# The last layer's modulation moved from attention's projections into the recurrence of the layer before

## The chip, the cores and the metric

One core of a Trainium2 chip runs the whole program. Five engines work side by side, each with its own queue in order: TensorE (PE; its weight loads are shown as PEld), VectorE (DVE), ScalarE (ACT), GpSimd (POOL) and SyncE (SP), which issues the DMAs. The metric is the device time of one execution in microseconds (us); less is better. The time of a kernel is the median of its runs.

## What is computed

A network of a first block and four layers over 512 tokens of width 1024, with 256 tokens of context beside them. The four layers are a gated convolution (0), an RWKV recurrence (1), attention (2) and a gated convolution again (3). Each layer has a modulation: shift, scale and gate, 3072 numbers for the token stream and 3072 for the context, from a vector that is the same in all layers.

```python
def modulation(cvec, w, b):
    m = jax.nn.silu(cvec) @ w + b          # cvec 1024, w 1024 x 3072
    return jnp.split(m, 3, axis=-1)

for i in range(4):
    shift, scale, gate = modulation(c, mod_w[i], mod_b[i])
    h = modulate(rmsnorm(x, norm_g[i]), shift[:, None], scale[:, None])
    ...                                     # layer i's branch gives y
    x = x + gate[:, None] * y
```

So the modulation of a layer depends on no layer before it, and can be computed at any time ahead of the layer that uses it. The modulation's weights are 12.6 MB a layer. Layer 1's recurrence runs over 12 blocks of 64 tokens, forward and backward at once:

```python
sa = jnp.einsum("bhvk,bhk->bhv", S, -kk_t)
S = (S * d_t[:, :, None, :] + sa[..., None] * (kk_t * a_t)[:, :, None, :]
     + v_t[..., None] * k_t[:, :, None, :])
out = jnp.einsum("bhvk,bhk->bhv", S, inp[5])
```

## The kernel before, in words

**The modulation.** A layer's 3072 columns are 24 blocks of 128. `mod_load` (line 597) loads one block of the weights, 512 KB, into a tile `mraw` of the pool `mods`, which has two buffers. `mod_mul` (lines 613 and 614) multiplies it: eight products of 128 x 32 by 128 x 128 in full fp32, four side by side in the columns of the array, and one ScalarE copy of the rows to `mrow`. After each four blocks `mod_cols` (lines 623 and 624) turns four rows into columns with four products, and VectorE adds the bias. `fill` does one such portion; `wblock`, which fetches and splits a block of any layer's weights, calls `fill` first, so the modulation is spread over a layer's weight blocks. `open_mods(to)` opens the pool and sets how far it goes; `close_mods` does what is left.

The layers 0 to 2 have their modulation computed in the first block and in the first convolution. Layer 3's is opened in `attn_layer`, just ahead of attention's projections, and interleaved with their 48 weight blocks. Its result is used only by the last convolution.

**The recurrence.** Each block j of 64 tokens needs four things in order: the scores (`scores`, line 1310, evicted by ScalarE as `Df`, line 1317, and by VectorE as `SK`, line 1319), a row recursion on VectorE that inverts small triangles (`rows`, lines 1343 and 1345), a block inverse on TensorE (`first`, line 1378, and `horner`, line 1387, from the tiles `T` and `M`), and the chain itself: `chain_v`, `chain_g` and `chain_u` (lines 1411, 1421, 1433) give U, which ScalarE and VectorE copy into `UV` (lines 1435 and 1436), `chain_s` (line 1443) makes the next state from it, `chain_o` (lines 1459 and 1466) the output. `step(j)` does the chain of block j, the block inverse of block j+1 and the scores and rows of block j+2, and starts the loads of `F` and `AR` of block j+3 (line 1284) and of V of block j+1 (line 1293). PSUM is split into two pools of four banks that go round: `pp` for scores, inverse and transposes, `pch` for the chain.

Steps -1 to 8 stand in `manual_schedule`: on each engine their instructions keep the order in which they are written. Steps 9 to 11, and all else, are ordered by a scheduler that simulates the program and gives each engine what is ready, by priority. Beside the last steps stand the normalization of one more row tile and the first weight blocks of the readout (`rwkv_w_o_2`), which starts with transposes on line 1654.

**Attention's projections.** 48 weight blocks of 512 KB are loaded (line 186), split by ScalarE and VectorE into a high and a low part (lines 170 and 173) and multiplied: keys, values and queries on lines 218 to 220, the gate on lines 199 to 202. The lines of the recurrence around the change are

```python
            sc(0, 1)
            if ch and j < 11:
                load_v(j + 1)
                for d in range(2):
                    chain_s(j, d)
```

Of the kernel before, what the change touches and what calls it, by code (L numbers as in the profile page):

```python
# [10 lines left out]
F32 = mybir.dt.float32  # L11
# [7 lines left out]
P = 128  # L19
# [15 lines left out]
WB=3  # L35
AP=[int(c) for c in "11"]
LT=2
MS=9
CB=4
CK=256  # L40
# [29 lines left out]
class K:  # L70
# [529 lines left out]
    def mod_mul(self):  # L600

        nc = self.nc
        i, j = divmod(self.mods_done, 24)
        self.mods_done += 1
        if j == 0:
            self.mods[i] = self.const.tile([P, 24, 2], F32, name=f"mod{i}")
        if j % 4 == 0:
            self.mod_rows = self.mpool.tile([P, 4, P], F32, name="mrow", bufs=1)
        raw = self.mraw.pop(0)
        ps = self.ptr.tile([P, 512], F32, name="tr")  # L610
        for k in range(KT):
            g = k % 4 * 32
            nc.tensor.matmul(ps[g:g + 32, 0:P], self.sc[:, k, :], raw[:, k, :], start=k < 4, stop=k >= 4)  # L613
        nc.scalar.activation(self.mod_rows[:, j % 4, :], ps[:, 0:P], AF.Copy)

    def mod_cols(self):

        nc = self.nc
        i, j = divmod(self.mods_out, 24)
        self.mods_out += 4  # L620
        ps = self.ptr.tile([P, 512], F32, name="tr")
        for q in range(4):
            nc.tensor.matmul(ps[:, 2 * q:2 * q + 2], self.mod_rows[:, q, :], self.msel, start=True, stop=True)
        nc.vector.tensor_tensor(self.mods[i][:, j:j + 4, :], ps[:, 0:8].rearrange("p (j s) -> p j s", s=2),
                                self.col("mod_b_2", 24 * i + j, 4).unsqueeze(2).to_broadcast([P, 4, 2]), ALU.add)

    def fill(self):

        if self.mods_done == self.mods_out + 4:
            self.mod_cols()  # L630
        if self.mods_read < self.mods_to:
            self.mod_load()
        if len(self.mraw) > 1 or self.mods_read == self.mods_to and self.mraw:
            self.mod_mul()

    def open_mods(self, to):

        self.mods_to = 24 * to
        self.mes = ExitStack()
        self.mpool = self.pool(self.mes, "mods", bufs=2, side="right")  # L640

    def close_mods(self):
        while self.mods_out < self.mods_to:
# [318 lines left out]
    def rwkv_layer(self, X, XC):  # L962
# [76 lines left out]
        def lerp_k(n, k, hi, lo):  # L1039
            t = stg.tile([P, WH], F32, name="l32", bufs=LT)  # L1040
            nc.vector.scalar_tensor_tensor(t, xx[:, k, :], self.col("rwkv_mu_2", 8 * n + k), h[:, k, 1:WH + 1],
                                           ALU.mult, ALU.add)
            self.split_x(hi, lo, t, True)
# [54 lines left out]
        def feat(name, i, shape=(P, 384)):  # L1098
            return fp.tile(list(shape), F32, name=name, bufs=FB[i])
# [3 lines left out]
        def done_k(p, t):  # L1103
            DQ(nc, 0).dma_start(k_d[p], t)
            sq = stg.tile([P, WH], F32, name="l32", bufs=LT)[:, :TA]
            hi, lo = [feat(nm, i, (P, WH))[:, :TA].bitcast(F32R) for nm, i in (("F", 5), ("AR", 6))]
# [180 lines left out]
        def load_v(j):  # L1287

            s = st[j]
            s.UV = []  # L1290
            for d in range(2):
                UV = B.pb.tile([P, H, 64], F32, name=f"UV{d}", bufs=2)
                nc.sync.dma_start(UV[hs[1 - d]].rearrange("p u v -> p (u v)"), vc_d[s.c[d] * 64:(s.c[d] + 1) * 64, :])
                nc.gpsimd.memset(UV[hs[d]], 0.0)
                s.UV.append(UV)
# [187 lines left out]
        def aside(j, i):  # L1483
            for _ in range(NAS[i][j]):
                next(normed, None)

        def step(j):

            ch, p2, p1 = j >= 0, 0 < j + 1 < 12, j + 2 < 12
            sc = (lambda d, g: scores(j + 2, d, g)) if p1 else (lambda d, g: None)  # L1490
            if p1:
                prep0(j + 2)
            if p2:
                expand(j + 1)
            if ch:
                G = chain_g(j)
            sc(0, 0)
            if ch:
                for hh in range(2):
                    chain_u(j, hh, G[hh])  # L1500
            sc(0, 1)
            if ch and j < 11:
                load_v(j + 1)
                for d in range(2):
                    chain_s(j, d)
            for g in range(4):
                if p2:
                    if g < 2:
                        first(j + 1, g)
                    else:  # L1510
                        horner(j + 1, 0, g - 2)
                if g % 2 == 0:
                    sc(1, g // 2)
                if g == 1:
                    if j + 3 < 12:
                        load(j + 3)
                    aside(j, 0)
            if p1:
                blocks(j + 2)
            for i in range(4):  # L1520
                if p2:
                    horner(j + 1, 1 + i // 2, i % 2)
                if p1:
                    rows(j + 2, max(1, 4 * i), 4 * i + 4)
                    tokens(j + 2, i // 2, i % 2)
                if ch and i < 3:
                    chain_o(j, i)
                if i == 2:
                    aside(j, 1)
            if p1:  # L1530
                back(j + 2)
            if j < 11:
                chain_v(j + 1)
            aside(j, 2)
# [48 lines left out]
        for nh in range(2):  # L1583
# [4 lines left out]
            def done_v(j, t, ps, nh=nh, lnb=lnb):  # L1588
# [7 lines left out]
                nc.vector.tensor_scalar(m, m, 1.0 / 64.0, None, ALU.mult)  # L1596
                vc = stg.tile([P, WH], F32, name="l32", bufs=LT)[:, :512].rearrange("p (h v) -> p h v", v=64)
                nc.vector.tensor_tensor(vc, p3, bc(m), ALU.subtract)
# [15 lines left out]
        zer = B.pb.tile([P, 512], mybir.dt.bfloat16, name="zer")  # L1614
        nc.gpsimd.memset(zer, 0.0)
        load_v(0)
        with tc.manual_schedule():
            for j in range(-1, MS):
                step(j)
            for _ in normed:  # L1620
                pass
        for j in range(MS, 12):
            step(j)
        lng = b0.tile([P, D], F32, name="lng", tag="SK00")
        nc.sync.dma_start(lng, ins["rwkv_ln_g_2"].rearrange("o n -> (o n)").partition_broadcast(P))
        for t in early[2:]:
# [9 lines left out]
        with ExitStack() as es:  # L1636
# [6 lines left out]
            for t in early + late:  # L1643
# [7 lines left out]
                for q in range(2):  # L1651
                    ps = self.ptr.tile([P, 512], F32, name="tr")
# [26 lines left out]
    def attn_layer(self, X, XC):  # L1679
# [7 lines left out]
        with ExitStack() as esl:  # L1687
# [7 lines left out]
            V = [kvp.tile([P, 6, HD], F32, name="V", bufs=8) for _ in range(8)]  # L1695
            rq = kvp.tile([P, 4, 16], F32, name="rq")
            kq = self.pool(esl, "atkq", bufs=2, side="right")
            self.open_mods(4)
            hds = [Ctx() for _ in range(16)]

            def split(hi, lo, x):
# [39 lines left out]
            with es_h:  # L1741
# [79 lines left out]
                for blk in range(8):  # L1821
                    gt = wk.tile([P, 2, T], F32, name="gt", tag="gt")
                    for m in range(2):
                        ps = self.mm()
# [1 line left out]
                        nc.scalar.activation(gt[:, m], ps, AF.Silu)  # L1826
                    nc.sync.dma_start(g_d[2 * blk:2 * blk + 2].rearrange("h d t -> d h t"), gt)

            self.close_mods()
            self.pes.close()  # L1830
            ylp = self.pool(esl, "atyl", bufs=8, side="right")
            with ExitStack() as es:
# [90 lines left out]
            with ExitStack() as es:  # L1923
# [3 lines left out]
                for nh in range(2):  # L1927
                    nsl = slice(nh * 512, (nh + 1) * 512)
                    self.linear_tm(w_out, nh * 512, lambda k: Gated(k, 0), lambda k: Gated(k, 1), TILES,
                                   lambda j, t, ps, nsl=nsl: self.residual(work, gate, X, j, nsl, ps), kts=16,  # L1930
# [141 lines left out]
```

## Time and profile before

| | us |
|---|---|
| median of 3 runs | 2657.45 |
| lowest and highest | 2656.79, 2659.92 |
| the profiled execution | 2661.63 |
| its span, first to last instruction | 2659.7 |
| TensorE busy | 2388.7 (90%) |
| VectorE, ScalarE, GpSimd busy | 1653.5, 1096.2, 589.7 |

The span is cut into stretches by the lines that run in them: the start of the recurrence from about 1240 us, the hand-ordered steps 0 to 8 up to about 1558, the last three steps up to 1638, the readout and attention's norm, and attention's projections from 1757 to 2096. A busy share says little by itself: what a stage is worth is read from what its last engine waits for.

### The profile page before, as it was taken

The numbers are of one execution on the slowest core, as the hardware profiler recorded it, in microseconds if no ns is written. First come the engines' busy times: TensorE is split into PE (matmuls) and PEld (weight loads), VectorE is DVE, ScalarE is ACT, GpSimd is POOL, SyncE is SP. The second block draws the span as 40 slices with busy tenths as digits, with TensorE's granted clock in tenths as the row PEclk, the third lists the DMA queues.
The fourth block names the chain that finished last, engine by engine and source line by source line (L and its number), as shares of the span: only waits on it lengthen the run. The fifth ranks groups of instructions, "written<-read, shape, count | busy, mean of one in ns | idle before, by whom it ended". The sixth has DMA issues, their size and how long they took to land. (4 is left out here: it accounts for less than half of the span.)

```text
span 2659.7 us, 48444 instructions
## 1 busy us (share of the span) xinstructions
PE 2388.7 (90%) x19868; PEld 1889.9 (71%) x19868; DVE 1653.5 (62%) x2580; ACT 1096.2 (41%) x2029; POOL 589.7 (22%) x544
## 2 busy tenths in 40 slices
PE   6998889899896889998799886989999899997997
PEld 4786667777575767666678775768788788876655
DVE  4434366995456478888788773554163478448836
ACT  4642353111434456653455552243233467432223
POOL 0101001000204046654232441110000387100001
PEclk8998899899997999997899997989999999998998
DMA  6533543434322237775433445242545311222331
GB/s 170 150 88 103 158 128 87 106 96 119 90 74 79 76 115 224 212 218 173 139 129 130 146 137 191 103 129 87 152 148 153 119 48 41 80 87 72 88 97 56
DMA packets 352941, 319.05 MB, mean 120 GB/s; under 512 B 19679, under 2 KB 292032, under 8 KB 352208
## 3 DMA queue, kind: packets, MB, share of 16 engines
q1 hardware_dynamic: 352720, 315.95, 39.6%
q8 instruction: 157, 2.57, 0.4%
q14 instruction: 64, 0.52, 0.1%
HBM read 241.85 MB, written 64.63 MB: 115 GB/s over the span
## 5 line engine op out<-in xcount | busy, mean ns | idle before, releaser
L173 DVE TENSOR_TENSOR wlo<-wraw,whi 128x1024 fp32r<-128x1024 f32 x212 | 263.6, 1244 | 460.9 <-ACT whi L170 453.4
L170 ACT ACTIVATE whi<-wraw 128x1024 fp32r<-128x1024 f32 x212 | 224.2, 1058 | 644.0 <-PE mm L200 336.0
L200 PE MATMUL mm<-hT_lo,whi 128*128 128x512 f32 (+1 forms) x864 | 323.5, 375 | 0.0
L199 PE MATMUL mm<-hT_hi,whi 128*128 128x512 f32 (+1 forms) x864 | 319.5, 381 | 2.5 <-ACT h L710 1.0
L202 PE MATMUL mm<-hT_hi,wlo 128*128 128x512 f32 (+1 forms) x864 | 290.7, 372 | 0.4 <-DVE wlo L173 0.4
L837 DVE SCALAR_TENSOR_TENSOR cvo<-ypad,dwh,cvo 128x784 f32<-128x784 f32 (+1 forms) x270 | 236.7, 906 | 4.7
L202 PEld LDWEIGHTS mm<-hT_hi,wlo 128*128 128x128 f32 x864 | 164.0, 190 | 40.6 <-issue 2.0
L199 PEld LDWEIGHTS mm<-hT_hi,whi 128*128 128x128 f32 x864 | 164.7, 191 | 38.6 <-issue 12.8
L200 PEld LDWEIGHTS mm<-hT_lo,whi 128*128 128x128 f32 x864 | 164.5, 191 | 32.7 <-issue 5.4
L218 PE MATMUL mm<-whi,hT_hi 128*128 128x512 f32 x384 | 152.6, 398 | 1.3 <-ACT hT_hi L263 1.3
L219 PE MATMUL mm<-wlo,hT_hi 128*128 128x512 f32 x384 | 152.3, 397 | 0.0
L220 PE MATMUL mm<-whi,hT_lo 128*128 128x512 f32 x384 | 150.1, 399 | 0.0
L797 POOL MEMSET ypad<- 128x15 f32 x16 | 1.8, 114 | 494.5 <-DVE cvo L837 272.1
L200 PE MATMUL mm<-llo,whi 128*128 128x256 f32 (+1 forms) x256 | 89.7, 368 | 11.3 <-DVE llo L273 11.3
L199 PE MATMUL mm<-lhi,whi 128*128 128x256 f32 (+1 forms) x256 | 85.0, 369 | 6.2 <-ACT lhi L270 6.2
L218 PEld LDWEIGHTS mm<-whi,hT_hi 128*128 128x128 f32 x384 | 72.5, 189 | 18.4 <-issue 1.8
L1317 ACT ACTIVATE Df<-ps 32x128 f32<-32x128 f32 x176 | 68.2, 387 | 37.9 <-PE ps L1310 35.7
L218 PE MATMUL mm<-whi,lhi 128*128 128x512 f32 x192 | 80.2, 424 | 4.0 <-DVE so L1566 3.2
L219 PEld LDWEIGHTS mm<-wlo,hT_hi 128*128 128x128 f32 x384 | 72.5, 189 | 15.6 <-issue 1.0
L220 PEld LDWEIGHTS mm<-whi,hT_lo 128*128 128x128 f32 x384 | 71.8, 189 | 16.5 <-issue 2.4
L613 PE MATMUL tr<-mraw,sc 128*32 128x128 f32 x1536 | 67.4, 291 | 16.8 <-DMA mraw<-in_mod_w_dram 13.6
L219 PE MATMUL mm<-wlo,lhi 128*128 128x512 f32 x192 | 79.9, 416 | 1.8 <-DVE wlo L173 1.8
(523 smaller groups left out, 5822.1 us busy)
## 6 DMA issues: line engine op xcount, KB each, us to landing
mraw<-in_mod_w_dram SPq DMA_DIRECT2D x96, 512.0 KB
wraw<-in_conv_w_in_dram SPq DMA_DIRECT2D x48, 512.0 KB
wraw<-in_attn_w_in_dram SPq DMA_DIRECT2D x48, 512.0 KB
wraw<-in_w_in_dram SPq DMA_DIRECT2D x24, 512.0 KB
f_d<-F SPq DMA_DIRECT2D x32, 384.0 KB
ar_d<-AR SPq DMA_DIRECT2D x32, 384.0 KB
F<-f_d SPq DMA_DIRECT2D x24, 512.0 KB
AR<-ar_d SPq DMA_DIRECT2D x24, 512.0 KB
```

Of the source, the lines that this page charges most:

```text
L170: nc.scalar.activation(hi[:, :n], raw, AF.Copy)
L173: nc.vector.tensor_tensor(lo[:, :n], raw, hi[:, :n].bitcast(F32), ALU.subtract)
L199: nc.tensor.matmul(ps[s], wh[:, k, :], xh(k)[:, a:b], start=k == 0, stop=False)
L200: nc.tensor.matmul(ps[s], wh[:, k, :], xl(k)[:, a:b], start=False, stop=False)
L202: nc.tensor.matmul(ps[s], wl[:, k, :], xh(k)[:, a:b], start=False, stop=k == kts - 1)
L218: nc.tensor.matmul(ps, h, wh[:, kk, :], start=k == 0, stop=False)
L219: nc.tensor.matmul(ps, h, wl[:, kk, :], start=False, stop=False)
L220: nc.tensor.matmul(ps, l, wh[:, kk, :], start=False, stop=k == kts - 1)
L613: nc.tensor.matmul(ps[g:g + 32, 0:P], self.sc[:, k, :], raw[:, k, :], start=k < 4, stop=k >= 4)
L797: nc.gpsimd.memset(yp_[:, 0:15], 0.0)
L837: nc.vector.scalar_tensor_tensor(acc, yp_[:, tap:tap + W], dwh[:, tap, kt:kt + 1], acc, ALU.mult, ALU.add)
L1317: nc.scalar.activation(s.Df[rows, :, :, gsl].rearrange("p t a u -> p u a t"), p3[rows, :, 32 * b:32 * b + 32].rearrange("p u (a t) -> p u ...
```

## The change

Layer 3's modulation is no longer opened in attention. It is opened just ahead of the recurrence's steps, with one buffer for `mraw` instead of two, and each step calls a new `fill_one` as often as a table `MODS` says, between the last scores of the first direction and the two state products. `fill_one` does, in this order, a due turn into columns, the product of the loaded block, and the load of the next. In the recurrence the products take their bank from the pool `pp`. One `fill_one` ahead of the steps only loads. The table gives two to step -1, one to each of steps 0 to 8, then three, five and five; a last call behind step 11 does the last turn.

```diff
+MODS=(2, 1, 1, 1, 1, 1, 1, 1, 1, 1, 3, 5, 5)
...
-        ps = self.ptr.tile([P, 512], F32, name="tr")
+        ps = self.mbank()
...
+    def mbank(self):
+        return self.ptr.tile([P, 512], F32, name="tr")
+
+    def fill_one(self):
+
+        if self.mods_done == self.mods_out + 4:
+            self.mod_cols()
+        if self.mraw:
+            self.mod_mul()
+        if self.mods_read < self.mods_to:
+            self.mod_load()
...
-    def open_mods(self, to):
+    def open_mods(self, to, bufs=2):
...
-        self.mpool = self.pool(self.mes, "mods", bufs=2, side="right")
+        self.mpool = self.pool(self.mes, "mods", bufs=bufs, side="right")
...
             if ch and j < 11:
                 load_v(j + 1)
+            for _ in range(MODS[j + 1]):
+                self.fill_one()
+            if ch and j < 11:
                 for d in range(2):
                     chain_s(j, d)
...
         load_v(0)
+
+        self.open_mods(4, 1)
+        self.mbank = lambda: bank("pp")
+        self.fill_one()
         with tc.manual_schedule():
...
         for j in range(MS, 12):
             step(j)
+        while self.mods_out < self.mods_to:
+            self.fill_one()
+        self.mes.close()
+        del self.mbank
...
             kq = self.pool(esl, "atkq", bufs=2, side="right")
-            self.open_mods(4)
...
-            self.close_mods()
             self.pes.close()
```

## Rows read from the trace of the kernel before

**Rows 1.** Busy time by stretch: length, busy us by engine, PEclk, DMA share, GB/s
```profile
1295.00:1558.00 263.00, 236.56 (x6357) 206.98 (x6353) 208.91 (x494) 142.46 (x329) 97.28 (x103) 0.94 0.41 132
1558.00:1638.00 80.00, 60.88 (x1693) 52.61 (x1691) 47.50 (x90) 32.16 (x68) 18.55 (x18) 0.89 0.33 103
...
1757.00:1990.00 233.00, 233.00 (x1394) 186.56 (x1393) 101.58 (x182) 77.65 (x206) 6.58 (x5) 1.00 0.43 126
1990.00:2096.00 106.00, 106.00 (x482) 87.62 (x480) 36.32 (x49) 35.47 (x51) 4.78 (x4) 1.00 0.52 154
```

**Rows 2.** Waits, 1757 to 2100: waiter <- releaser, us, times, longest (PE, ACT)
```profile
PE sc L1857 <- ACT gt L1826: 1.5, 1, 1.5
...
ACT whi L170 <- PE mm L220: 84.5, 29, 8.3
```

**Rows 3.** Timeline of PE in the projections: start, us, line, operation, count
```profile
1867.28 0.39 PE L220 MATMUL mm<-whi,hT_lo 128*128 128x512 f32 x1
1867.51 0.39 PE L218 MATMUL mm<-whi,hT_hi 128*128 128x512 f32 x1
1867.83 0.64 PE L613 MATMUL tr<-mraw,sc 128*32 128x128 f32 x16
1868.40 0.50 PE L219 MATMUL mm<-wlo,hT_hi 128*128 128x512 f32 x1
1868.74 0.40 PE L220 MATMUL mm<-whi,hT_lo 128*128 128x512 f32 x1
...
1910.58 0.40 PE L220 MATMUL mm<-whi,hT_lo 128*128 128x512 f32 x1
1910.81 0.95 PE L623 MATMUL tr<-msel,mrow 128*128 128x2 f32 x8
...
1912.27 0.50 PE L218 MATMUL mm<-whi,hT_hi 128*128 128x512 f32 x1
```

**Rows 4.** Groups of PE by line, 1757 to 2096: count, busy us, mean ns
```profile
L613 PE MATMUL tr<-mraw,sc 128*32 128x128 f32 x384 | 15.5, 279 | 0.0
L623 PE MATMUL tr<-msel,mrow 128*128 128x2 f32 x48 | 6.4, 241 | 0.0
```

**Rows 5.** PE waits, 1290 to 1560, and step 2's DVE and PE timeline
```profile
PE ps L1443 <- DVE UV L1436: 20.2, 16, 5.3
...
1363.59 1.29 DVE L1319 TENSOR_TENSOR SK<-ps,kcb 128x512 f32<-128x512 f32 x2
1364.91 1.30 DVE L1436 COPY UV<-ps 64x512 f32<-64x512 f32 x2
...
1363.36 1.15 PE L1443 MATMUL ps<-UV,BK 128*64 128x64 f32 x32
1365.65 0.33 PE L1443 MATMUL ps<-UV,BK 128*64 128x64 f32 x2 [1.14 <-DVE UV L1436]
```

**Rows 6.** Timeline of SP's queue: a step's first load, the next step's store
```profile
1385.14 0.61 SPq L1284 DMA_DIRECT2D F<-f_d  x1
...
1411.11 1.12 SPq L1471 DMA_DIRECT2D o_d<-Os  x2
```

**Rows 7.** Timeline at the recurrence's start, PE and DVE
```profile
1272.93 4.52 PE L1310 MATMUL ps<-AR,F 64*128 64x128 f32 x34 [7.74 <-DMA AR<-ar_d]
...
1290.28 0.70 DVE L1333 STREAM_TRANSPOSE Nt<-Df 128x512 f32<-128x512 f32 x1
...
1306.66 2.57 PE L1443 MATMUL ps<-UV,BK 128*64 128x64 f32 x32 [5.26 <-DVE UV L1436]
```

**Rows 8.** Timeline of the first block: a modulation load and the product behind it
```profile
52.64 6.57 SPq L597 DMA_DIRECT2D mraw<-in_mod_w_dram  x3
...
57.71 1.08 PE L613 MATMUL tr<-mraw,sc 128*32 128x128 f32 x16 [4.27 <-DMA mraw<-in_mod_w_dram]
```

**Rows 9.** Timeline of PE behind step 9: where it waits
```profile
1597.13 2.40 PE L1378 MATMUL ps<-T,SK 64*64 64x64 f32 x40 [5.70 <-POOL T L1371]
...
1616.26 0.31 PE L1387 MATMUL ps<-CX,M 64*32 64x32 f32 x2 [6.17 <-DVE CX L1393]
...
1647.12 1.94 PE L1654 MATMUL tr<-ident,ro 128*128 128x128 f32 x8 [11.23 <-DMA ro<-y_d]
```

More of the change, by code (lines that the diff above doesn't have):

```diff
@@ L620, in mod_cols @@
         self.mods_out += 4
-        ps = self.ptr.tile([P, 512], F32, name="tr")
+        ps = self.mbank()
         for q in range(4):
```

## The prediction

> **What bounds the kernel now.** I read the stages first, then the waits of the engine that is full, then single instructions around the work that moves. The stretch table [rows 1] shows two kinds of stage. In attention's projections (1757 to 2096 us) TensorE is busy for the whole of both stretches, 233.00 of 233.00 and 106.00 of 106.00, at the full clock (1.00, so 2.4 GHz). In the nine steps of the recurrence that stand in a hand-written order (1295 to 1558) it is busy 236.56 of 263, and in the last three steps, which the scheduler orders (1558 to 1638), 60.88 of 80. The waits [rows 2] say who is last: in the projections TensorE waits once, for 1.5 us; ScalarE, which splits the weights, waits 84.5 us in 29 waits until TensorE has left a weight buffer. So there the weights are ahead, and every TensorE instruction lies on the path that sets the end. In the recurrence no engine is full, so what an added instruction costs depends on the gap it falls into.
>
> **Part 1, what leaves attention.** The last layer's modulation is 24 blocks: one load of 512 KB, eight products (16 records, since each stands as two), one ScalarE copy; and after each four blocks four products (eight records) that turn rows into columns, and one small VectorE add. The count is 384 records and 48 [rows 4], so 24 blocks and six turns. Their durations overlap, so I take the displacement from the start times [rows 3]. Matmuls of the projection start 0.23 us apart (1867.28, 1867.51). Around one block the next starts at 1868.40, 0.89 later, 0.66 more than 0.23; the one behind starts 0.34 later, 0.11 more; the next few are some 0.01 late each, 0.05 in all. That is 0.82 a block. Around a turn and a block together it is 1912.27 - 1910.58 = 1.69, which is 0.80 more than 0.89, so 0.75 to 0.80 a turn. Sum: 24 x 0.82 + 6 x 0.75 = 19.7 + 4.5 = 24.2 us off a stage that waits for nothing. Next late would be the weights, and [rows 2] shows them waiting for TensorE, so I expect all of it, with 22 and 25 as ends for turns that the records show broken in two. ScalarE and VectorE lose the copies and adds too; neither was last.
>
> **Part 2, nine steps in the written order (j = 0 to 8).** Each step gains one block before the two state products (chain_s), two of them a turn as well (j = 2 and 6). TensorE idles just there: 20.2 us in 16 waits for VectorE's copy of U into UV [rows 5]. In step 2 the state products of the second direction wait 1.14 us until 1365.65. The block takes a bank of the pool of four that go round; the one that it gets was last that of the step's first score group, and VectorE frees it after the first SK product at about 1364.2 (1.29 us for two from 1363.59). So the block runs at 1364.2 to 1364.9, the first state products (1.15 us, they stood before the wait) move behind it to 1366.0, and the second ones find both UV copies done at 1366.2. Cost: about nothing; with a turn in the same step some 0.7 more, since 0.82 + 0.75 is over the wait. I take 1 us for all nine; the ends are 0 and 9 x 0.82 + 2 x 0.75 = 8.9, if the cover were gone.
>
> The block's ScalarE copy lies in the gap before M and costs nothing. The load is another matter: the pool has one buffer, so **SP** waits at the next load until TensorE has done the product. Behind that load on SP's queue stand the four F and AR loads of block j+3 (2 MB), later the norm's loads and the output store. They are issued at 1385.14 now, just after the store of the step before, and would be issued some 8 us later; they are wanted when the next step's scores start, behind the next store at 1411.11 [rows 6]. Some 16 us are left for 2.5 MB, so I cost it at nothing; if it didn't fit, TensorE would wait at the first scores.
>
> **Part 3, the start (j = -1).** Two blocks stand here, between the first direction's scores of block 1 and the second's. The first one's load goes out with the other first loads. The second load can only go out when the first product is done, and its product stands in the written order ahead of the second direction's scores. From an early stretch [rows 8]: a load issued at 52.64 has its product at 57.71, 5.07 later, and TensorE waited 4.27 of it. The first scores start at 1272.93 [rows 7]; the first product then falls near 1277.5, the second near 1283, and the remaining scores and their evictions end near 1290.5 to 1292. What waits for them is VectorE's transpose, now at 1290.28, and behind it the row recursion that VectorE bounds in step 0 (TensorE waits 5.26 us at 1306.66). So a delay goes straight through. I take 2 us, ends 0 (the scheduler puts block 0's own products into the wait) and 7 (5.07 and two products at half clock).
>
> **Part 4, the last three steps and behind them.** Thirteen blocks (3, 5, 5) and four turns. As TensorE work they are 13 x 0.82 + 4 x 0.75 = 13.7 us; TensorE idles 80 - 60.88 = 19.1 us here [rows 1], 5.70 of it at 1597.13 behind the T tile, 6.17 at 1616.26, and another 11.23 before 1647.12, where the readout begins [rows 9]. But the blocks are a chain, one buffer: product, load, product. At 5.07 from issue to product and 0.64 for the product it is 5.7 us a block, 74 us for thirteen, against 80 us and the 11.23 behind them. It fits, barely. Where it pinches: a later tile of the four-bank pool waits for the copy of the block four tiles before it, so in step 9 the second half of "first" waits for the third block, and the last blocks should fall into the gap before 1647. Part of the work lies ahead of scores on which the VectorE recursion of block 11 depends (the 5.70 shows that this one is last in step 10), and that part is paid. I take 6 us, nearer to the middle than to either end, since about half the gaps lie behind a chain that the blocks themselves push; the ends are 0 and 13.7.
>
> **A rule against it.** The row is the 4.27 us for which TensorE stood still between two blocks that had no other work between them [rows 8]. The Trainium skill, "Trainium Kernel Development and Optimization", section Best Practices, says to double-buffer so that DMA overlaps compute; this change goes from two buffers to one. By that rule the thirteen blocks would pay the transfer in the open; by the row they pay only where nothing else is queued. What it gives is the second rival.
>
> **Sum.** -24.2 + 1 + 2 + 6 = -15.2 us. The profiled execution took 2661.63 us, with a span of 2659.7; less 15.2 that is 2646.4. The median of the runs is 2657.45, 4.2 below it, so I predict 2657.45 - 15.2 = 2642.2, say 2642 us.
>
> **The rivals.**
> First, the gain is eaten in the last three steps: the bank rotation holds "first" and "horner" behind blocks that wait for loads, and SP, waiting with a load, holds the output stores or the readout's weights behind it. For it: the chain of 74 us has hardly room, and 6.17 us at 1616.26 show that the scheduler already misjudges this stretch. Against it: 19.1 + 11.23 us of gaps. Price 14 to 25 instead of 6: 2657.45 - 24.2 + 3 + 19 = 2655, within 0.2%.
> Second, on the other side: one buffer puts the transfer on TensorE's queue. TensorE is in order; where the scheduler has put a block too early, everything behind it waits, up to 4.27 us each. Place: steps 9 to 11. Price for all thirteen 13 x 4.27 = 55.5, so 2657.45 - 24.2 + 3 + 55.5 = 2692; it decides from about five whole waits on (5 x 4.27 = 21.3, all that is left of the gain after 3). For it: steps 10 and 11 hold ten blocks, a chain of 57 us in some two thirds of the 80. Against it: other products are ready in most of that time. Eight whole waits give 2670.
> Third, the change doesn't shorten attention, as the projections turn out bound by the weights' loads: 2657.45 + 9 = 2666. Against it: [rows 2].
> Fourth, a better case of the forecast: the tail hides all, 2657.45 - 24.2 + 3 = 2636.
>
> **How the numbers follow.** A measurement of this kernel can tell about 0.2%, 5.3 us, from no change. The forecast with its better case gets 0.66, the first rival 0.19, the second 0.12, the third 0.03. So faster 0.66, same 0.19, slower 0.15. Likeliest time 2642. The low end has all of Part 1 at 25 and nothing paid: 2632. The high end has 22 + 7 + 8.9 + 13.7 as 2665 with all ends at once; I stop at 2662, which takes in the first rival and leaves out most of the second and third.
>
> **What would show it.** The projections, from the first weight product to the first score of a head, should be 22 to 25 us shorter, still without waits of TensorE. From the first scores of block 1 to the store of step 8 the time should grow by 1 to 5 us, with the waits before the state products shrunk. The last three steps should grow by some 6, with the blocks seen in the gaps; waits of TensorE for mraw there speak for the second rival, waits of "first" or "horner" for ScalarE's mrow copy for the first. I am wrong if attention shrinks by less than 20, or the recurrence grows by more than 15.

## The result, and the profile after

The changed kernel takes **2670.98 us** (median of 4 runs, 2668.21 to 2674.27) against 2657.12 us of the kernel before, measured beside it (4 runs). The ratio is 1.0055, with a 95% interval of 1.004 to 1.0071. The forecast of 2642 and its range up to 2662 were wrong, and on the wrong side: the change makes the kernel slower by 14 us.

The stages show at once where. Each is measured between two landmarks in the two profiled executions (2661.63 us before, 2674.27 after): SP's load of the constants `kcb`, VectorE's first transpose `Nt` of block 1, the store of step 8, the first transpose of the readout, the first product of attention's projections, the first score of a head.

| stage | before | after | difference | forecast |
|---|---|---|---|---|
| up to the `kcb` load | 1237.9 | 1236.1 | -1.8 | 0 |
| start, to `Nt` | 52.4 | 58.2 | +5.8 | +2 (0 to 7) |
| steps, to the store of step 8 | 267.9 | 271.9 | +4.0 | +1 (0 to 8.9) |
| last three steps, to the readout | 89.0 | 113.4 | **+24.4** | +6 (0 to 13.7) |
| readout and norm | 105.1 | 105.0 | 0 | 0 |
| projections, to the first score | 345.5 | 321.1 | **-24.4** | -24.2 |
| the rest | 562.0 | 566.5 | +4.5 | 0 |

The prediction's signs of being wrong were a gain of less than 20 us in attention, which did not come, and a recurrence longer by more than 15: it is 34 us longer. The first and the last stage hold no line of the change. In the eleven kernels below, whose code there is the same too, the last one is 562.6 to 571.1, so in one profiled execution a difference of some 4 us is not read as an effect.

**The projections gave what they were to give.** This is the stretch view of the kernel after, with the columns of [rows 1]: the steps, the last three steps, the projections.

```profile
1299.00:1566.00 267.00, 237.37 (x6444) 207.38 (x6441) 211.61 (x498) 142.96 (x334) 97.95 (x103) 0.94 0.46 150
1566.00:1670.00 104.00, 76.56 (x1910) 63.88 (x1908) 49.27 (x93) 35.64 (x80) 18.54 (x18) 0.85 0.46 136
1789.00:2104.00 315.00, 315.00 (x1447) 261.33 (x1445) 137.39 (x223) 107.91 (x231) 11.81 (x9) 1.00 0.36 108
```

TensorE is busy for all of the 315.00 us at the full clock, with 1447 records; before it was 339 us with 1394 + 482 = 1876 [rows 1]. The difference of 429 is about the 384 + 48 records of the modulation [rows 4]. The weights did not become the bound: the view of waits for that stretch names none of TensorE for a weight, and ScalarE still waits until a weight buffer is left, as in [rows 2].

```profile
ACT whi L172 <- PE mm L222: 88.1, 27, 9.3
```

**In the nine ordered steps the product took the place of the wait.** TensorE's waits, 1290 to 1566 us (waiter <- releaser: us in total, times, longest):

```profile
PE ps L615 <- DVE SK L1333: 16.3, 6, 8.0
...
PE ps L625 <- DVE SK L1333: 2.8, 2, 1.9
```

The 20.2 us of waiting for `UV` ahead of the state products [rows 5] are gone. The modulation's product (L615) and turn (L625) stand there instead and wait 16.3 + 2.8 us for their bank, which VectorE frees with `SK`; no score waits for the loads of `F` and `AR`, which in step 3 go out 10.4 us behind the store (1397.03 against 1386.64) where it was 2.8 before.

**In the last three steps TensorE waits for the load, and once for ScalarE.** TensorE's waits, 1555 to 1700 us:

```profile
PE ps L615 <- DMA mraw<-in_mod_w_dram: 18.6, 8, 5.7
PE ps L1447 <- ACT G L1439: 8.3, 1, 8.3
```

The wait for `G` is not one for a load. On ScalarE the normalization of a row tile, which waits for GpSimd, stands ahead of the second copy `G`; in the kernel before it stands behind both copies and waits for nothing:

```profile
1614.67 1.06 ACT L1247 ACTIVATE rx<-rx 128x1024 f32<-128x1024 f32 x1 [7.92 <-POOL rx L1244]
1615.63 0.58 ACT L1439 ACTIVATE G<-ps 128x512 f32<-128x512 f32 x1
```

The timeline shows what stands behind the waits for the load (start, length, engine, operation, count, and in brackets the idle time before it and its releaser):

```profile
1606.05 0.64 PE L615 MATMUL ps<-mraw,sc 128*32 128x128 f32 x16
...
1640.73 1.08 PE L615 MATMUL ps<-mraw,sc 128*32 128x128 f32 x16 [5.74 <-DMA mraw<-in_mod_w_dram]
1641.74 3.36 PE L1392 MATMUL ps<-T,SK 64*64 64x64 f32 x58
...
1655.77 1.08 PE L615 MATMUL ps<-mraw,sc 128*32 128x128 f32 x16 [1.51 <-DMA mraw<-in_mod_w_dram]
...
1661.16 0.64 PE L615 MATMUL ps<-mraw,sc 128*32 128x128 f32 x16 [0.90 <-DMA mraw<-in_mod_w_dram]
1661.73 0.57 PE L1473 MATMUL ps<-UV,SK 128*64 128x64 f32 x12
...
1666.95 1.08 PE L615 MATMUL ps<-mraw,sc 128*32 128x128 f32 x16 [3.80 <-DMA mraw<-in_mod_w_dram]
1667.97 0.90 PE L1480 MATMUL ps<-S,AR 64*64 64x64 f32 x18
1672.03 1.08 PE L615 MATMUL ps<-mraw,sc 128*32 128x128 f32 x16 [3.16 <-DMA mraw<-in_mod_w_dram]
```

The block inverse of block 11 (L1392, "first") runs at 1641.74 only, behind a product that waited 5.74 us for its tile. What it needs from GpSimd was there long before, at 1612.34:

```profile
1610.11 2.23 POOL L1385 TENSOR_SCALAR T<-Xq,kcb 128x512 f32<-128x512 f32 x2
```

In the kernel before, the inverse started as soon as `T` was there (1597.13, [rows 9]). Here it is 29.4 us later. In the text of a step the blocks of the modulation stand ahead of the inverse, and both take their banks from `pp`; in every kernel below with blocks in step 10 the inverse runs behind the last of them. So the chain of loads sets when block 11 is inverted, and block 11 is the last of the chain. And the last output (L1473, L1480) is cut into pieces by products that wait again. The last four products stand 5.39, 5.79 and 5.08 us apart. The product with the longest wait came 8.09 us behind the issue of its load (1632.64), which shared the DMA engines with two weight loads of the readout (issued from 1630.59) and an output store (from 1633.11). SP waits with the loads all that time, but the last store is issued at 1669.84, right behind ScalarE's output copy (from 1668.73), so here it is TensorE that is late and not SP:

```profile
1641.87 26.58 SPq L599 DMA_DIRECT2D mraw<-in_mod_w_dram  x5
1669.84 1.09 SPq L1485 DMA_DIRECT2D o_d<-Os  x2
```

### The profile page after: what moved, and what is told of

The parts are those of the page before. It is cut to its first block, busy times and chain, and to the rows that moved or that the text cites. A ratio compares the mean times of both kernels' runs of the same rounds, so it can differ in the third digit from the quotient of the medians.

```text
span 2672.3 us, 48430 instructions
## 1 busy us (share of the span) xinstructions
PE 2383.0 (89%) x19868; PEld 1890.4 (71%) x19868; DVE 1659.2 (62%) x2580; ACT 1098.1 (41%) x2029; POOL 589.8 (22%) x544
## 5 line engine op out<-in xcount | busy, mean ns | idle before, releaser
L222 PE MATMUL mm<-whi,llo 128*128 128x512 f32 x192 | 79.7, 421 | 3.0 <-DVE llo L275 3.0
```

Source lines behind the costliest of these rows:

```text
L222: nc.tensor.matmul(ps, l, wh[:, kk, :], start=False, stop=k == kts - 1)
```

## The experiments

Blocks of the modulation are counted by where they stand: at the start (step -1), in the steps 0 to 8, in the last three steps (9, 10, 11), and left in attention. "Buffers" are those of `mraw` from step 9 on. The start and the tail are the stages of the table above, in the profiled execution; "busy" is TensorE's busy time in the tail, and "mraw" what it waited there for the modulation's loads.

| run | start / steps / tail / left | buffers | us | ratio to before, interval | start | tail | busy | mraw |
|---|---|---|---|---|---|---|---|---|
| before | 0 / 0 / 0 / 24 | | | 1 | 52.4 | 89.0 | 60.7 | |
| after | 2 / 9 / 3+5+5 / 0 | 1 | 2670.98 | 1.0055, 1.0040 to 1.0071 | 58.2 | 113.4 | 79.2 | 18.6 |
| e1_steps | 0 / 8 / 0 / 16 | | 2658.62 | 1.0014, 1.0003 to 1.0025 | 53.4 | 96.3 | 61.7 | |
| e2_start | 2 / 6 / 0 / 16 | | 2659.33 | 1.0016, 1.0006 to 1.0025 | 58.0 | 90.8 | 60.8 | |
| e3_tail | 0 / 0 / 3+5+4 / 12 | 1 | 2676.96 | 1.0080, 1.0063 to 1.0098 | 52.4 | 109.1 | 75.0 | 13.1 |
| e4_deep | 2 / 9 / 3+5+5 / 0 | 3 | 2654.74 | 0.9991, 0.9978 to 1.0004 | 58.1 | 101.7 | 74.4 | 4.0 |
| e8_two | 2 / 9 / 3+5+5 / 0 | 2 | 2659.48 | 1.0012, 1.0002 to 1.0023 | 58.3 | 101.4 | 72.4 | 5.2 |
| e5_noload | 2 / 9 / 3+5+5 / 0 | no loads | 2644.86 | 0.9961, 0.9946 to 0.9975 | 58.0 | 93.3 | 72.5 | 0 |
| e6_late | 0 / 9 / 5+5+5 / 0 | 3 | 2658.76 | 1.0014, 1.0004 to 1.0025 | 53.4 | 110.2 | 78.6 | 8.4 |
| e7_half | 0 / 9 / 1+1+1 / 12 | 3 | 2649.15 | 0.9978, 0.9968 to 0.9988 | 52.5 | 87.7 | 62.8 | 0 |
| e9_early | 0 / 9 / 8+7+0 / 0 | 3 | **2645.96** | 0.9958, 0.9946 to 0.9970 | 53.2 | 100.2 | 76.6 | 5.7 |
| e10_two3 | 0 / 9 / 4+3+0 / 8 | 3 | 2668.07 | 1.0046, 1.0033 to 1.0058 | 53.4 | 107.1 | 69.3 | 2.9 |
| e11_one | 0 / 9 / 8+7+0 / 0 | 1 | 2690.00 | 1.0120, 1.0103 to 1.0137 | 52.3 | 142.5 | 89.3 | 35.4 |

My theory after the result (A) was the second rival: one buffer makes the tail a chain of load, product and load, and TensorE, in order, stands still with it (in the expectations SP, which waits with the loads, is part of it). The rivals were that TensorE's added work, the banks and ScalarE's copies make the tail long (B), and, from the first four runs on, that the scheduler finds another order for the tail whatever is put into it (C). A further theory, that loads in step 11 hold the readout's weights back (D), came with e9_early.

### Each part alone: e1_steps, e2_start, e3_tail

Only the table of places differs, and what isn't in it stays in attention.

```diff
-MODS=(2, 1, 1, 1, 1, 1, 1, 1, 1, 1, 3, 5, 5)
+MODS=(0, 1, 1, 1, 1, 1, 1, 1, 1, 1, 0, 0, 0)
...
         self.open_mods(4, 1)
+        self.mods_to = 72 + 8
```

> Eight blocks, one in each of the steps 0 to 7 with two turns, none at the start and none behind step 8; the other sixteen stay in attention with two buffers. Theory A (the last three steps ate the gain: 24 us between the store of step 8 and the readout): attention gives back 8 x 0.82 + 2 x 0.75 = 8.1 us, the steps cost the 4.3 us that the traces show between the stores of step 0 and step 8, so some 4 us below the kernel before, about 2653. Theory B (a block in the recurrence costs as much wherever it stands, since banks and order are disturbed): 2660 or more.

Measured: 2658.62 us. That is neither theory's time: 5.6 us over A's and 1.4 under B's. The projections are 337.8 us, 7.7 shorter than before, as eight blocks and two turns should make them. The start (53.4) and the ordered steps (265.4) cost nothing. But the tail, in which no block stands, is 96.3 us instead of 89.0. TensorE's waits in it, 1555 to 1655 us:

```profile
PE ps L1392 <- POOL T L1385: 6.7, 2, 6.4
PE ps L1447 <- ACT G L1439: 4.2, 2, 3.5
PE ps L1457 <- ACT UV L1449: 3.9, 1, 3.9
```

ScalarE's copies `G` and `UV` come late, since the scheduler put other work ahead of them: the normalization of a row tile that waits for GpSimd, and a split of a readout weight that waits for its load.

```profile
1595.61 1.06 ACT L1247 ACTIVATE rx<-rx 128x1024 f32<-128x1024 f32 x1 [11.41 <-POOL rx L1244]
...
1598.17 1.06 ACT L1439 ACTIVATE G<-ps 128x512 f32<-128x512 f32 x2
1605.02 1.06 ACT L172 ACTIVATE whi<-wraw 128x1024 fp32r<-128x1024 f32 x1 [5.79 <-DMA wraw<-in_rwkv_w_o_dram]
1605.98 0.57 ACT L1449 ACTIVATE UV<-ps 64x512 f32<-64x512 f32 x1
```

So the blocks in the steps are free, and the gain of eight was lost in a tail whose order moved although nothing was added to it.

```diff
+MODS=(2, 1, 1, 1, 1, 1, 1, 0, 0, 0, 0, 0, 0)
```

> The same eight blocks, but two of them in step -1 and six in the steps 0 to 5, as the change has them; sixteen in attention. If the start is what the traces show (VectorE's transpose Nt 6.2 us later against the first loads), 5 to 6 us more than the run with none at the start, about 2659. If the start is hidden: 2653.

Measured: 2659.33 us. With two blocks at the start this stage is 58.0 us, 4.6 more than in e1_steps, about as expected. But the total is only 0.7 us more than there, since the tail, again without a block in it, is 90.8 and not 96.3. So the expected total came, but not by the expected difference.

```diff
+MODS=(0, 0, 0, 0, 0, 0, 0, 0, 0, 0, 3, 5, 4)
...
+        self.mods_to = 72 + 12
```

> Twelve blocks in the last three steps only (3, 5, 4, one buffer), the other twelve in attention. Theory A: attention gives 12 x 0.82 + 3 x 0.75 = 12.1 us, the last steps cost some 22 to 24, so about 2668. Theory B, or the start as the culprit: the last steps cost no more than their share, 2645 to 2652.

Measured: 2676.96 us, the slowest of the three by far, although the projections are 12.0 us shorter (333.5). The start (52.4) and the steps (267.9) are those of before; the tail grows by 20.1 us, with 13.1 us of waiting for `mraw`. So the tail's loss needs nothing of the other parts. The total is 9 us over what A gave, and the tail does not explain that: the stage behind the first score is 571.1 us here instead of 562.0, and why stays open.

### More buffers: e4_deep, e8_two, and none to wait for: e5_noload

From step 9 on two tiles of the pool of `F`, no longer used there, serve as further buffers for `mraw`, and the loads run as far ahead.

```diff
...
+        while self.mods_read < self.mods_to and len(self.mraw) < self.mdepth:
             self.mod_load()
...
+        own, turn = self.mtile, [0]
+
+        def mtile():
+            turn[0] += 1
+            tag = ('F00', 'F10', None)[turn[0] % 3]
+            return b0.tile([P, KT, P], F32, name="mraw", tag=tag) if tag else own()
+
+        self.mdepth, self.mtile = 3, mtile
+        while self.mods_read < self.mods_to and len(self.mraw) < self.mdepth:
+            self.mod_load()
         for j in range(MS, 12):
             step(j)
```

> The change, with three buffers for the weights of the blocks behind step 8 (two of them tiles of F that are free by then) and the loads issued as far ahead. If the cost of the last steps is the chain through one buffer (TensorE waits 18.6 us for mraw there, and SP stands with a load ahead of the last output store): the waits go, 2652 to 2656. If it is the banks, the added products or the order itself: 2666 to 2671, with the waits moved to other lines.

Measured: 2654.74 us, 16 less than with one buffer, and no longer to be told from the kernel before. The waits for `mraw` fall from 18.6 to 4.0 us, the tail from 113.4 to 101.7. The wait for `G` behind the normalization is still there, 6.7 us, so it is not what the buffers took away. What they shortened is the way to the inverse of block 11: the five products of step 10 are done at 1617.24, and the inverse starts 11.6 us behind its `T`, not 29.4.

```profile
1605.34 2.20 POOL L1390 TENSOR_SCALAR T<-Xq,kcb 128x512 f32<-128x512 f32 x2
1619.09 0.83 PE L1397 MATMUL ps<-T,SK 64*64 64x64 f32 x10
```


The same with one tile more than the change's:

```diff
+            tag = ('F00', None)[turn[0] % 2]
...
+        self.mdepth, self.mtile = 2, mtile
```

> The change with two buffers instead of one from step 9 on (the second is a tile of the F pool that is no longer used there). Theory A: a block comes round every (5.07 + 0.64) / 2 = 2.9 us, 37 us for thirteen in the 80 us of the last steps, so the chain no longer binds: total 2654 to 2658, tail some 102 us, hardly worse than with three buffers. If the wait grew in proportion to what is left of the chain (half of it at two buffers), 2662. Theory B: 2667 to 2671.

Measured: 2659.48 us; waits 5.2 us, tail 101.4. The second buffer takes away most of what the third does, as the chain of 2.9 us a block would have it, but the time is 1.5 us over what A gave; in the profiled execution a turn waits 5.7 us for ScalarE's copy of the rows.

In e5_noload the 13 products of the tail all take the tile that is in the buffer then, and nothing is loaded behind step 8; its output is not the reference's.

```diff
-        raw = self.mraw.pop(0)
+        raw = self.mraw[0] if self.keep else self.mraw.pop(0)
...
-        if self.mods_read < self.mods_to:
+        if self.mods_read < self.mods_to and not self.keep:
             self.mod_load()
...
+        self.keep = True
         for j in range(MS, 12):
             step(j)
```

> The change as it is, but behind step 8 no block is loaded: the 13 blocks of the last three steps all multiply the one tile that stands in the buffer then, so most columns of the modulation are not the reference's. TensorE's added work, the banks, ScalarE's copies and the order of the text stay. Theory A (the chain load, product, load through one buffer, and SP behind it, cost 16 of the 24 us by which the tail grew): the tail, from the store of step 8 to the readout, falls from 113 to 102 us or less, total 2650 to 2656. Theory B (the bank rotation or the added TensorE work cost it, and the deeper buffers of the earlier run helped by another way): the tail stays above 110, total 2667 to 2671.

Measured: 2644.86 us, 26 us below the change and 5 below what A expected. The tail is 93.3 us, only 4.3 more than before, and holds a wait of 6.4 us for `G` as the change does; the inverse of block 11 starts 11.2 us behind its `T`. The stretch view of the tail (columns as in [rows 1]) is a balance of TensorE's time. Before:

```profile
1558.14:1647.12 88.98, 60.74 (x1693) 52.65 (x1692) 47.40 (x90) 32.02 (x67) 18.55 (x18) 0.86 0.38 116
```

After:

```profile
1566.23:1679.62 113.39, 79.22 (x1932) 66.32 (x1932) 49.21 (x94) 35.68 (x80) 18.54 (x18) 0.82 0.49 146
```

Without loads (e5_noload):

```profile
1563.52:1656.81 93.29, 72.47 (x1933) 61.88 (x1932) 49.45 (x95) 35.09 (x80) 18.55 (x18) 0.89 0.38 112
```

The same 1932 or 1933 records make 72.47 us of work without the loads and 79.22 with them: the granted clock is 0.89 in the one, 0.82 in the other (72.47 x 0.89 / 0.82 = 78.7). Idle is what is left of the length: 28.2 us before, 20.8 without loads, 34.2 after. So without loads 11.7 us of work come in and 7.4 of them go into gaps, and 4.3 stay. With the loads 18.5 us come in, no gap is used, and 5.9 us of idling are added. The loads' share of the tail's growth, 20.1 of 24.4 us, is 13.4 of idling and 6.7 of the same work at a lower clock.

### Where the blocks stand: e6_late, e7_half, e9_early, e10_two3, e11_one

All five have nothing at the start and one block in each of the steps 0 to 8; the first four have the three buffers of e4_deep.

```diff
+MODS=(0, 1, 1, 1, 1, 1, 1, 1, 1, 1, 5, 5, 5)
```

> No block at the start (0 instead of 2), one in each of the steps 0 to 8, fifteen (5, 5, 5) in the last three with three buffers. Against the change with three buffers (2654.7): the start gives back 5.8 us, the two further blocks of the tail cost 2 x 0.82 = 1.6, so 2650.5, ratio 0.997 to 0.999. Theory C (the order that the scheduler finds for the tail moves by itself by some 7 us with any edit): 2645 to 2660, with the difference in the tail and not at the start; the start would still be 52.4 us from the kcb load to the first transpose.

Measured: 2658.76 us. The start is 53.4 us again, but the tail takes 110.2, and the sum is 8 us off; only theory C's wide range holds it. What comes last is not TensorE. It ends step 11 at 1647.4 us and then waits 20.13 until the readout; in the kernel before that wait was 11.23 [rows 9].

```profile
1638.40 17.08 SPq L188 DMA_DIRECT2D wraw<-in_rwkv_w_o_dram  x6
1655.54 1.11 SPq L1490 DMA_DIRECT2D o_d<-Os  x2
```

```profile
1650.79 1.06 ACT L172 ACTIVATE whi<-wraw 128x1024 fp32r<-128x1024 f32 x1 [3.85 <-DMA wraw<-in_rwkv_w_o_dram]
1652.78 1.06 ACT L172 ACTIVATE whi<-wraw 128x1024 fp32r<-128x1024 f32 x1 [0.93 <-DMA wraw<-in_rwkv_w_o_dram]
1653.74 1.07 ACT L1488 ACTIVATE Os<-ps 128x512 f32<-128x512 f32 x2
```

The blocks' loads stand ahead of the readout's weight loads on SP, which go out from 1638 to 1655 us, where it was 1606 to 1621 in the kernel before. ScalarE splits those weights ahead of the last output copy `Os`, so the copy and the store behind it wait for weights that nobody needs yet. This is the first rival's mechanism, SP with a load ahead of other transfers, and three buffers don't take it away.

```diff
+MODS=(0, 1, 1, 1, 1, 1, 1, 1, 1, 1, 1, 1, 1)
...
+        self.mods_to = 72 + 12
```

> Half of the change: twelve blocks in the recurrence (none at the start, one in each step, three buffers from step 9 on), twelve left in attention. Attention gives 12 x 0.82 + 3 x 0.75 = 12.1 us, the nine ordered steps cost about 1, the last three 3 x 0.82 + 0.75 = 3.2 at most: total 2647 to 2651 from 2657. Theory C (the scheduler's order of the tail moves by itself, as in the run with eight blocks, where step 10 grew by 7 us with no block in it): 2652 to 2657, with the loss in steps 9 to 11 and waits there for other engines and not for loads.

Measured: 2649.15 us, ratio 0.9978 (0.9968 to 0.9988): half of the change, where it costs nothing, is faster than before by the amount that the sum gave. The tail is 87.7 us.

```diff
+MODS=(0, 1, 1, 1, 1, 1, 1, 1, 1, 1, 8, 7, 0)
```

> All 24 blocks in the recurrence: none at the start, one in each of the steps 0 to 8, eight in step 9, seven in step 10, none in step 11, three buffers from step 9 on. Theory D (with three buffers, what is left of the loss is SP's order: the blocks' loads of step 11 stand ahead of the output layer's weight loads, ScalarE's splits of these weights then stand ahead of the last output copy): without loads in step 11 the tail falls from 110 (5, 5, 5) towards the 93 of the run without loads, some 94 to 100; total 2657 - 24.2 + 1 + 5 to 11 = 2639 to 2645. Theory C (the order of the tail moves by itself): tail 100 to 112, total 2649 to 2660.

Measured: **2645.96 us**, ratio 0.9958 (0.9946 to 0.9970): all 24 blocks moved, and 25 us faster than the change; it lies between the two theories, 1 us over D's range and 3 under C's. The readout's weights go out at 1617.73 and from 1624.12 to 1633.15, and ScalarE is through with its splits of the tail by 1631.5, well ahead of the copy of the last output at 1644.74. The tail is 100.2 us, at the upper end of theory D and the lower one of C. The order on ScalarE is a good one as well: both copies `G` stand ahead of the normalization that waits for GpSimd.

```profile
1602.29 0.60 ACT L1444 ACTIVATE G<-ps 128x512 f32<-128x512 f32 x1 [3.19 <-PE ps L1440]
1603.34 0.60 ACT L1444 ACTIVATE G<-ps 128x512 f32<-128x512 f32 x1 [0.46 <-PE ps L1440]
...
1610.49 1.06 ACT L1252 ACTIVATE rx<-rx 128x1024 f32<-128x1024 f32 x1 [5.84 <-POOL rx L1249]
```

```diff
+MODS=(0, 1, 1, 1, 1, 1, 1, 1, 1, 1, 4, 3, 0)
...
+        self.mods_to = 72 + 16
```

> Sixteen blocks in the recurrence (one in each of the steps 0 to 8, four in step 9, three in step 10, none in step 11, three buffers from step 9 on), eight left in attention. Attention gives 16 x 0.82 + 4 x 0.75 = 16.1, the ordered steps cost 1, the tail by theory D the products alone, 7 x 0.33 (4.3 us over 13 in the run without loads) + 1 = 3: total 2645, tail 89 to 93. Theory C: tail 95 to 105, total 2650 to 2656.

Measured: 2668.07 us, a miss of 23 us, and with fewer blocks in the tail than e9_early. The waits for `mraw` are 2.9 us; what TensorE waits for in the tail is ScalarE:

```profile
PE ps L1406 <- ACT M L1398: 11.2, 2, 10.3
...
PE ps L1452 <- ACT G L1444: 10.7, 1, 10.7
```

```profile
1604.48 1.06 ACT L1252 ACTIVATE rx<-rx 128x1024 f32<-128x1024 f32 x1 [11.41 <-POOL rx L1249]
...
1607.04 1.06 ACT L1444 ACTIVATE G<-ps 128x512 f32<-128x512 f32 x2
...
1626.55 1.06 ACT L172 ACTIVATE whi<-wraw 128x1024 fp32r<-128x1024 f32 x1 [3.86 <-DMA wraw<-in_rwkv_w_o_dram]
1627.51 0.58 ACT L1398 ACTIVATE M<-ps 128x512 f32<-128x512 f32 x1
```

Here the normalization stands ahead of `G` and the weight splits ahead of `M`: 22 us of waiting, none of it for a load of the modulation (the last one in the tail was issued by 1574). Theory D is not what decides here; theory C's size was too small.

```diff
-MODS=(2, 1, 1, 1, 1, 1, 1, 1, 1, 1, 3, 5, 5)
+MODS=(0, 1, 1, 1, 1, 1, 1, 1, 1, 1, 8, 7, 0)
```

Against the change only the table differs, so this is e9_early with one buffer.

> All 24 blocks in the recurrence, none at the start, one in each of the steps 0 to 8, eight in step 9, seven in step 10, none in step 11, but one buffer as in the change. Against the same places with three buffers (2645.96, tail 100.2). Theory A (the chain of load, product, load through one buffer costs by itself, wherever the blocks stand): fifteen blocks at 5.7 us are 85 us, against some 70 until step 10 ends, so TensorE's waits for the tile return to 15 us or more, the tail grows to 113 or more, total 2659 to 2668. Theory D (it was only that the loads of step 11 stood on SP ahead of the last store and of the weight loads): tail 100 to 104, total 2646 to 2650.

Measured: 2690.00 us, 44 us more than with three buffers at the same places. A's mechanism holds wherever the blocks stand; its size was given too small (2659 to 2668). TensorE waits 35.4 us for `mraw`:

```profile
PE ps L615 <- DMA mraw<-in_mod_w_dram: 35.4, 11, 6.5
```

and the balance of its tail, against that of e9_early, is

```profile
1554.68:1697.21 142.53, 89.28 (x1984) 74.58 (x1985) 47.59 (x91) 36.68 (x82) 19.11 (x18) 0.73 0.41 123
```

```profile
1555.40:1655.62 100.22, 76.55 (x1977) 64.81 (x1985) 49.40 (x95) 35.99 (x82) 19.01 (x18) 0.88 0.58 174
```

Idle 53.3 against 23.7 us, and the same work 12.7 us longer at a granted clock of 0.73 instead of 0.88. In neither does TensorE wait behind the normalization for `G`. The inverse of block 11 starts 33.3 us behind its `T` with one buffer and 11.1 with three.

## Why the prediction was wrong

**Part 1 was right.** 24.4 us left the projections against 24.2, and parts of it go with their share to about 2 us (7.7 in e1_steps and 9.7 in e2_start for eight blocks and two turns, 12.0 and 13.8 in e3_tail and e7_half for twelve and three). The displacement from the start times [rows 3] was the right price, and the lack of waits of TensorE [rows 2] the right reason. The third rival is out.

**Part 2 was right.** The steps are 271.9 us after against 267.9, but over the eleven kernels of the experiments that stage is 265.1 to 271.6, on both sides of before, so the blocks there cost no more than can be seen. The trace shows the exchange that the step named: the waits for `UV` gave way to waits of the product for its bank.

**Part 3 was mis-sized.** The start cost 5.8 us, where I took 2 and 7 as the end. It repeats: 58.0 to 58.3 us in the five kernels with two blocks there, 52.3 to 53.4 in the eight without, that of before among them. TensorE's and then SP's timeline at the start, after:

```profile
1274.66 1.08 PE L615 MATMUL ps<-mraw,sc 128*32 128x128 f32 x16
1279.90 3.68 PE L1392 MATMUL tr<-T,SK 64*64 64x64 f32 x64 [4.16 <-POOL T L1385]
1283.51 0.41 PE L615 MATMUL ps<-mraw,sc 128*32 128x128 f32 x2
...
1285.41 0.64 PE L615 MATMUL ps<-mraw,sc 128*32 128x128 f32 x14
1285.98 0.49 PE L1324 MATMUL ps<-AR,F 64*128 64x128 f32 x2
...
1289.71 1.39 PE L1324 MATMUL ps<-AR,F 64*128 64x128 f32 x20
```

```profile
1275.80 10.68 SPq L599 DMA_DIRECT2D mraw<-in_mod_w_dram  x2
```

`Nt` follows at 1294.34 (1290.28 before). Block 0's own products did go into the wait for the second load, as I said; but I counted that as cover. They stand ahead of the second product in TensorE's order, one of them waits 4.16 us for GpSimd, and the remaining scores, on which `Nt` depends, start only at 1285.98. The second product ends 10.2 us behind the issue of its load, not 5.07 + 0.64. The transfer was not what held it. This is the busy share of the DMA engines from 1275 to 1281 us in 40 slices of 0.15 us:

```profile
DMA  3010400000002595799999998520000000000000
```

What they move in the busy slices, 0.52 MB, is this load. Its bytes are in by 1279.05, 4.5 us before the product starts at 1283.51, just as the block inverse ahead of it ends. The term left out is the order: a wait for GpSimd, and behind it the inverse, ahead of the second product and so of the scores.

**Part 4 is the step that failed**: 24.4 us, where I took 6 and the whole work, 13.7, as the end. "It fits, barely" compared a sum of lengths (13 x 5.7 = 74) with a length (80 + 11). The period was right: 5.39, 5.79 and 5.08 us between the last products. But the chain does not run all the time. Its first product is at 1575.6, 9.4 us behind the store of step 8, and between the third (1586.1) and the fourth (1606.05) TensorE's order has none for 20 us; ten blocks are left from there on, 57 us at the least, and the last product is issued at 1672. The end of 13.7 left out that a product which waits blocks all that stands behind it, and this was no unknown: it stands in the second rival. "Other products are ready in most of that time" was the reason for its small chance. They were ready but stood behind, on an engine in order. The one that counts is the inverse of block 11: I had seen in the 5.70 us that this path is last in step 10, but not that the inverse would stand behind all five blocks of that step, 29.4 us behind its `T`. Nor did the period hold for every block: the longest wait belongs to a load that took 8.09 us beside other transfers. Eight waits came, as the rival's example had it, but of 18.6 us in all and not eight whole ones (34.2), and idling also lowered the clock under the rest of the work, which no term of the sum had. And 8.3 us are the wait for `G`, an order on ScalarE that no term had either. The rival gave 2670 at eight waits, beside the measured 2671. That is its mechanism but luck in the number: with 18.6 us of waits its own sum is 2655, and it has neither the 18.5 us of added busy time in the tail nor more than 2 of the 5.8 at the start.

The rule that I cited from the Trainium skill, "Trainium Kernel Development and Optimization", section Best Practices, to double-buffer so that DMA overlaps compute, agrees with this case: at the same places three buffers instead of one took 16 us off (e4_deep) and 44 us (e11_one against e9_early).

**The first rival** was right in one half. It had "first" held behind blocks that wait for loads, and that is where the inverse of block 11 stood. Its sign, a wait of "first" or "horner" (L1392, L1401) for a copy `mrow`, is not in the tail, so whether the rotation of the banks or only the scheduler's order keeps the inverse behind the blocks is not shown; no run gave the blocks banks of their own or put them behind the inverse in the text. Its other half, SP, was not what cost the time: SP does wait with the loads (1641.87 to 1668.45), but the last store is not late by it. More buffers take away SP's waits together with TensorE's, so that it was TensorE is read from the timeline. SP's half is seen in e6_late, where the readout's weights are late and ScalarE with them.

**What stays open.** The tail's order on ScalarE changes with every edit, by waits of some 8 us (e1_steps) to 22 us (e10_two3) behind two foreign steps, the normalization of a row tile and the weight splits. No run held that order fixed, so part of each difference between two tails is the scheduler's. It doesn't carry the verdict on the buffers, which was asked at two sets of places and on a kernel without loads, with one sign, and between kernels that agree in the wait for `G` (8.3, 6.7 and 6.4 us in the change, e4_deep and e5_noload, none in e9_early and e11_one); but whether e9_early is good for its places or for its order can't be told apart here.

## What to carry to other kernels

Before a load and its product are moved into another stage, write down for each product when its tile can be there and what stands behind it on its in-order engine, the work that the next stage needs above all: a total that fits in the length of the stage says nothing if the chain can't start early or has holes. Give moved loads at least as many buffers as they had, and ask of each queue that issues them what else it will hold back. And where a scheduler orders the stage, try several placements: the same work cost 2646 or 2659 us with two tables of places, and half of it 2649.

## What the runs showed of the hardware

The tail that waited paid twice. In e11_one against e9_early, with 1984 and 1977 records of the same products, TensorE idled 53.3 us against 23.7, and its granted clock was 0.73 against 0.88; its busy time grew by 12.7 us. In the timeline of the kernel after, the product of one block took 1.07 or 1.08 us behind the five longest of its eight waits for the load, and 0.64 or 0.65 behind the three shortest. But the length of the wait alone does not decide it: in e11_one eight of the eleven waits, one of 0.91 us among them, are followed by a product of 1.08 us, and the three of 2.11, 2.16 and 3.65 us by one of 0.64 or 0.65.

From the issue of a load of 512 KB to its product, where the product waited for it, it took 3.9 to 5.1 us for the last four blocks of the kernel after (5.07 in [rows 8]) and 8.09 us where weight loads and a store were under way. At the start the bytes were in 3.25 us behind the issue, and the product was done only 10.2 us behind it, since other products stood ahead of it.
